# Mixer A: the delta rule's matrix reads the key gram from an SBUF copy instead of a second set of matmuls

## The chip, the cores and the metric

One core of one Trainium2 chip runs one inference step of a two-layer diffusion backbone. The metric is the device time of the core in microseconds. Shown are the median of three runs and one further execution that the hardware profiler recorded. Engines are named as in the profile: PE is TensorE's matmul stream, PEld its weight loads, DVE is VectorE, ACT is ScalarE, POOL is GpSimd, SP is SyncE, whose queue issues the DMAs here.

## The reference, cut to what matters

640 tokens (128 of context, 512 latent) go through an even and an odd layer. In the even layer `p = h @ w_in` feeds eight gated-DeltaNet heads (mixer A) beside eight attention heads (mixer B), and both results go through `w_out`. A DeltaNet head works in chunks of 64 tokens, in two directions:

```python
def l2norm(x): return x * rsqrt(sum(x * x, -1) + EPS)
q = l2norm(q) * DK_A ** -0.5 ; k = l2norm(k)
...
decay = exp(where(tri, gc[..., :, None] - gc[..., None, :], NEG))
kb = k * beta[..., None]
lmat = where(strict, einsum('bhncd,bhnsd->bhncs', kb, k) * decay, 0.0)
tmat = lmat + eye(CHUNK)
u = triangular_solve(tmat, v * beta) ; w = triangular_solve(tmat, kb * exp(gc))
attn = where(tri, einsum('bhncd,bhnsd->bhncs', q, k) * decay, 0.0)
```

Three 64x64 products of each chunk matter here: keys with keys (for `lmat`), keys with queries (for `attn`), and the diagonals of keys with keys and of queries with queries (for the two norms). Keys and queries enter all of them without their norms; those are multiplied in later, per token.

## The kernel before, in words

**The big matmuls.** The projection of the even layer is cut into 53 blocks of 128 output features. `Main` works them off: a block has four quarters, a quarter's weights come by a DMA on SP's queue (`w_st`), are split by ACT into a high part (`w_hi`, L1049) and by DVE into a low part (`w_lo`, L1051), and are multiplied three times with the activations (`acc<-hh,w_hi`, `acc<-hl,w_hi`, `acc<-hh,w_lo`), 320 tokens at a time.

**The order on PE.** `run` puts the instructions of PE in an order written down at build time. Every mixer is a generator. A `yield` of a number asks to be continued that much later, by a planner's clock `g.now`, in which a matmul counts a fixed price (`G.mm`; ten products of a gram count 0.53 us together). Whenever no generator is due, `Main.step` emits a few of the big matmuls. PE keeps exactly this order; the instructions of the other engines are ordered by the compiler's own scheduler, within their data dependencies, and may be moved ahead of others there. Each engine then works strictly in its order.

**A head of mixer A.** `prep` takes the blocks of keys and queries, runs the short convolution (`a_conv`) and then `a_prep`, which the change touches. `a_prep` first asks for the gram of keys with keys and that of queries with queries: ten 64x64 products each, written by PE to a PSUM tile `a_gram`. DVE multiplies it with a unit matrix into half of the tile `a_M` or `a_at` (L268) and sums it (L269); that gives the norms. Norms, gates and decays then become small per-token factors on DVE, and the decay matrices `a_M` and `a_at`, made by DVE (L308, L309), ACT (L310, L311) and POOL (L300, L301, L314). After `yield LAT["gram"]` (9 us of planner time) PE computes keys with keys into a new `a_gram`, DVE multiplies it into `a_M` (L320), and `a_invert` sends `a_M` through DRAM to POOL (SP's queue, L481 and L484), which inverts triangles of 32x32 in 30 dependent pairs of steps. Then PE computes keys with queries, and DVE multiplies that into `a_at` (L320 again). About 50 us later the inverse is loaded (`a_inverted`), put together (`a_join`, tile `i_vps`), and `a_scan` walks the ten chunk steps of the head (tiles `a_st`, `a_vns`, `a_vno`, `a_s`). The scan of one head and the preparation of the next overlap, and both overlap the attention heads of mixer B (tiles `at_s`, `at_pt`, `at_o`).

**PSUM.** In this stage the eight banks are: three for `acc`, three for the scan, and two that everything else shares in turn (tag `"gen"`): `a_gram`, `at_s`, `at_pt`, `at_o`, `i_vps`, the transposes, and `ada_ps` of a side stream (`g.aside`) that computes modulations inside the scan. A new user of that pair waits until the last but one has been read.

Of the kernel before, what the change touches and what calls it, by code (L numbers as in the profile page):

```python
# [8 lines left out]
F32 = mybir.dt.float32  # L9
# [80 lines left out]
def rsqrt(g, pool, x, n, tag, bufs=1):  # L90

    nc = g.nc
    y = pool.tile([128, n], F32, name=f"{tag}_y", tag=f"{tag}_y", bufs=bufs)[0:x.shape[0]]
    t = pool.tile([128, n], F32, name=f"{tag}_t", tag=f"{tag}_t")[0:x.shape[0]]
    yi = y.bitcast(I32)
    nc.vector.tensor_scalar(out=yi, in0=x.bitcast(I32), scalar1=1, scalar2=None, op0=ALU.logical_shift_right)
    nc.vector.tensor_scalar(out=yi, in0=yi, scalar1=-1.0, scalar2=float(0x5F3759DF), op0=ALU.mult, op1=ALU.add)
    for _ in range(3):
        nc.vector.tensor_mul(t, y, y)
        nc.vector.scalar_tensor_tensor(out=t, in0=t, scalar=-0.5, in1=x, op0=ALU.mult, op1=ALU.mult)  # L100
        nc.vector.scalar_tensor_tensor(out=y, in0=t, scalar=1.5, in1=y, op0=ALU.add, op1=ALU.mult)
    return y
# [137 lines left out]
def a_prep(g, h, qT, kT):  # L240

    nc, c, A = g.nc, g.c, g.A
    W, P1 = g.paw, g.pa1
    U = [128, 2, 5]
    hs = lambda t: t[:, :, :, h]
    bc = lambda t, n: t.unsqueeze(3).to_broadcast([128, 2, 5, n])


    df = W.tile([128, 10, 64], F32, name="a_df", bufs=1)
    for lo, hi in HALVES:  # L250
        nc.sync.dma_start(df[lo:hi], g.gcd[:, :, h, lo:hi].rearrange("o b s -> (o b) s").unsqueeze(0).to_broadcast([64, 10, 64]))
    b10 = lambda t: t.unsqueeze(2).to_broadcast([128, 10, 64])
    at = g.pe.tile([128, 2, 5, 64], F32, name="a_at", tag="a_at", bufs=2)
    M = P1.tile([128, 2, 5, 64], F32, name="a_M")
    def gram(x):

        ps = g.psg.tile([128, 5, 64], F32, name="a_gram", tag="gen")
        for b in range(5):
            for hf in range(2):
                cc = b * 128 + hf * 64  # L260
                g.mm(ps[hf * 64:hf * 64 + 64, b], lhsT=x[0][:, cc:cc + 64], rhs=x[1][:, cc:cc + 64], start=True, stop=True,
                     tile_position=(0, hf * 64))
        return ps

    ss = W.tile([128, 2, 5], F32, name="a_ss")
    for i, (x, sq) in enumerate(((kT, M), (qT, at))):
        ps = gram((x, x))
        nc.vector.tensor_tensor(out=sq[:, 0], in0=ps, in1=c["i64"].unsqueeze(1).to_broadcast([128, 5, 64]), op=ALU.mult)  # L268
        nc.vector.tensor_reduce(out=ss[:, i], in_=sq[:, 0], op=ALU.add, axis=mybir.AxisListType.X)  # L269
        yield  # L270
    sse = W.tile([128, 2, 5], F32, name="a_sse")
    nc.vector.tensor_scalar_add(sse, ss, 4 * EPS)
    rr = rsqrt(g, W, sse.rearrange("p a b -> p (a b)"), 10, "a_rr", bufs=2)
    rk, rq = rr[:, 0:5], rr[:, 5:10]
    rkb = rk.unsqueeze(1).to_broadcast(U)

    sm = lambda n: W.tile(U, F32, name=n, bufs=2)
    fm = c["fm"].rearrange("p (o b) -> p o b", o=2)
    bm = c["bm"].rearrange("p (o b) -> p o b", o=2)
    a = W.tile(U, F32, name="a_a")  # L280
    rk2 = W.tile([128, 5], F32, name="a_rk2")
    nc.vector.tensor_mul(rk2, rk, rk)
    nc.vector.tensor_mul(a, hs(A["beta"]), rk2.unsqueeze(1).to_broadcast(U))
    p2 = sm("a_p2")
    nc.vector.tensor_mul(p2, bm, sse[:, 0].unsqueeze(1).to_broadcast(U))
    nc.vector.tensor_add(p2, p2, hs(A["bfm"]))
    nc.vector.scalar_tensor_tensor(out=p2, in0=p2, scalar=0.5, in1=rkb, op0=ALU.mult, op1=ALU.mult)
    p1 = sm("a_p1")
    nc.vector.tensor_mul(p1, a, fm)
    nc.vector.tensor_add(p1, p1, bm)  # L290
    nc.vector.scalar_tensor_tensor(out=p1, in0=p1, scalar=-1.0, in1=hs(A["egc"]), op0=ALU.mult, op1=ALU.mult)
    c1 = sm("a_c1")
    nc.vector.tensor_mul(c1, a, bm)
    nc.vector.tensor_add(c1, c1, fm)
    c2 = sm("a_c2")
    nc.vector.tensor_mul(c2, c1, hs(A["dl"]))


    d4 = df.rearrange("p (o b) s -> p o b s", o=2)
    nc.gpsimd.tensor_tensor(out=d4, in0=d4, in1=bc(hs(A["gc"]), 64), op=ALU.subtract)  # L300
    nc.gpsimd.tensor_tensor(out=at, in0=df.rearrange("p (o b) s -> p o b s", o=2),  # L301
                            in1=c["maskA"].rearrange("p (o s) -> p o s", o=2).unsqueeze(2).to_broadcast([128, 2, 5, 64]),
                            op=ALU.add)
    Mu = M.rearrange("p o b s -> p (o b) s")
    for o, (lo, hi) in enumerate(HALVES):
        f, b = slice(o * 5, o * 5 + 5), slice(5 - o * 5, 10 - o * 5)
        ms = c["maskS"][lo:hi].unsqueeze(1).to_broadcast([64, 5, 64])
        nc.vector.scalar_tensor_tensor(out=Mu[lo:hi, f], in0=df[lo:hi, f], scalar=-1.0, in1=ms, op0=ALU.mult, op1=ALU.add)  # L308
        nc.vector.tensor_tensor(out=Mu[lo:hi, b], in0=df[lo:hi, b], in1=ms, op=ALU.add)  # L309
    nc.scalar.activation(M, M, AF.Exp)  # L310
    nc.scalar.activation(at, at, AF.Exp)  # L311
    an = W.tile([128, 10], F32, name="a_an")
    nc.vector.tensor_scalar_mul(an, a.rearrange("p o b -> p (o b)"), -1.0)
    nc.gpsimd.tensor_tensor(out=Mu, in0=Mu, in1=b10(an), op=ALU.mult)  # L314


    yield LAT["gram"]
    for dst, x in ((M, kT), (at, qT)):
        ps = gram((kT, x))
        nc.vector.tensor_tensor(out=dst, in0=ps.unsqueeze(1).to_broadcast([128, 2, 5, 64]),  # L320
                                in1=dst, op=ALU.mult)
        if dst is M:
            inv = a_invert(g, M)
        yield
    return dict(h=h, qT=qT, kT=kT, inv=inv, at=at, p1=p1, p2=p2, c1=c1, c2=c2, rq=rq)
# [149 lines left out]
def a_invert(g, M):  # L475

    nc, W, P1 = g.nc, g.paw, g.pa1
    d1 = g.pd.tile([6, 10, 32, 32], F32, name="inv_in", tag="inv_in")
    for q in range(4):
        sub = q % 2  # L480
        nc.sync.dma_start(d1[q].rearrange("u i j -> i u j"),  # L481
                          M[q * 32:q * 32 + 32].rearrange("p o b s -> p (o b) s")[:, :, sub * 32:sub * 32 + 32])
        if sub == 1:
            nc.sync.dma_start(d1[4 + q // 2].rearrange("u i j -> i u j"),  # L484
                              M[q * 32:q * 32 + 32].rearrange("p o b s -> p (o b) s")[:, :, 0:32])
    SY = P1.tile([128, 1024], F32, name="i_S").rearrange("p (i j) -> p i j", i=32)
    S, Yt = SY[0:40], SY[64:104]
    nc.sync.dma_start(S, d1[0:4].rearrange("q u i j -> (q u) i j"))
    E = nc.gpsimd
    E.memset(S.rearrange("p i j -> p (i j)")[:, 0:1024:33], 1.0)  # L490
    for j in range(1, 31):
        n = 31 - j
        t = P1.tile([40, 240], F32, name="i_tmp", bufs=2)[:, 0:n * j].rearrange("p (a b) -> p a b", a=n)
        E.tensor_tensor(out=t, in0=S[:, j + 1:, j].unsqueeze(2).to_broadcast([40, n, j]),  # L494
                        in1=S[:, j, 0:j].unsqueeze(1).to_broadcast([40, n, j]), op=ALU.mult)
        E.tensor_tensor(out=S[:, j + 1:, 0:j], in0=S[:, j + 1:, 0:j], in1=t, op=ALU.add)  # L496
    Y = S
    E.tensor_tensor(out=Yt, in0=Y.rearrange("p i j -> p j i"), in1=g.c["ones"][0:40, 0:32].unsqueeze(1).to_broadcast([40, 32, 32]),
                    op=ALU.mult)
    d2 = g.pd.tile([2, 4, 10, 32, 32], F32, name="inv_out", tag="inv_out")  # L500
    nc.sync.dma_start(d2[0].rearrange("q u i j -> (q u) i j"), Y)
    nc.sync.dma_start(d2[1].rearrange("q u i j -> (q u) i j"), Yt)
    return d1, d2
# [1044 lines left out]
def body(nc, tc, I, O):  # L1548
    off = [(k, v.shape[1]) for k, v in const_table().items()]
    with ExitStack() as es:  # L1550
# [100 lines left out]
        with ExitStack() as e1:  # L1651
# [25 lines left out]
            def prep():  # L1677
                for h in range(8):
                    yield lambda: st["joined"] >= h - 2
                    k = a_conv(g, h, 1, (yield from get(8 + h, 0.5)))  # L1680
                    yield lambda: st["scanned"] >= h - 2
                    q = a_conv(g, h, 0, (yield from get(h, 0.5)))
                    yield LAT["conv"]
                    yield lambda: st["gates"]
                    prepped[h] = yield from a_prep(g, h, q, k)
                    st["ready"][h] = g.now
# [299 lines left out]
```

## Time and profile before

| | before |
|---|---|
| median of three runs | 2717.81 us (2716.46 to 2723.16) |
| the profiled execution | 2723.34 us, span 2721.5 us |
| mean granted PE clock | 0.983 |
| busy: PE, PEld | 2601.2 us (96%), 2435.2 us (89%) |
| busy: DVE, ACT, POOL | 1536.9 us (56%), 954.0 us (35%), 704.9 us (26%) |
| matmuls of `a_gram` | 640 of 21303, between 189.3 and 974 us |
| mixers A and B | from about 180 to 1240 us |

A busy share is an average over the whole span. PE's matmuls overlap one another, so the time that a group costs is read from the distance of the starts, not from the sum of the durations. A row of the timeline gives start, duration, engine, line, instruction, `out<-in`, shape and count; the brackets at its end say how long the engine had been idle before it and who ended the wait. In the trace one of the kernel's fp32 products shows as two matmul records, so a gram of ten products shows as 20.

### The profile page before, as it was taken

How to read it: one execution, taken by the hardware profiler on the slowest of the kernel's cores; microseconds unless marked ns; L12 is line 12 of the kernel's file. 1: busy time of each engine (PE TensorE's matmuls, PEld its weight loads, DVE VectorE, ACT ScalarE, POOL GpSimd, SP SyncE). 2: the span in 40 equal slices, each digit the busy share in tenths (PEclk: the TensorE clock that was granted, in tenths of full speed). 3: DMA queues.
4: the chain of work that ended last, by engine and by line, in shares of the span. 5: the costliest groups of instructions: out<-in, count | busy, mean ns of one | idle time of the engine just before them, and what ended most of it. 6: DMA issues, size and time to landing. Idle time of an engine off the chain costs nothing.

```text
span 2721.5 us, 54637 instructions
## 1 busy us (share of the span) xinstructions
PE 2601.2 (96%) x21303; PEld 2435.2 (89%) x21303; DVE 1536.9 (56%) x3598; ACT 954.0 (35%) x2150; POOL 704.9 (26%) x894
## 2 busy tenths in 40 slices
PE   6989999999999999999999899999999999999996
PEld 4779788988978997799998899999999999998996
DVE  5766546656556565357876755546453644545225
ACT  3232343433433343442224443343333434233222
POOL 2326514253251550001223330012001301221113
PEclk9989999999999999999999999999999999999998
DMA  9932434243243424246653413323232222325324
GB/s 334 309 97 71 116 95 122 81 133 116 85 126 111 123 60 136 72 143 200 214 186 115 127 64 105 106 76 97 81 108 90 87 93 87 98 69 183 99 97 136
DMA packets 264706, 329.85 MB, mean 121 GB/s; under 512 B 76013, under 2 KB 148925, under 8 KB 264447
## 3 DMA queue, kind: packets, MB, share of 16 engines
q1 hardware_dynamic: 264447, 326.35, 38.2%
q8 instruction: 168, 2.75, 0.4%
q14 instruction: 91, 0.75, 0.1%
HBM read 294.95 MB, written 28.68 MB: 119 GB/s over the span
## 4 chain that ended last, share of the span: by engine, by line
PE 44%; DVE 3%; DMA 2%; issue 1%; ACT 0%; DVEq 0%; SPq 0%; ACTq 0%
PE acc L77 38%; PE at_s L77 1%; PE at_o L77 1%; DMA vec<-w_ada 1%; PE c_lv L77 1%; DVE hl L1774 1%; DVE vec L1320 1%; PE c_ops L77 1%; PE tm_ps L84 1%; PE c_U L77 0%; DVE x L1427 0%; PE at_pt L84 0%; DVE w_lo L1051 0%; PE c_bp L77 0%; DMA hl<-o_d 0%
## 5 line engine op out<-in xcount | busy, mean ns | idle before, releaser
L77 PE MATMUL acc<-hh,w_hi 128*128 128x320 f32 (+1 forms) x4544 | 1446.7, 319 | 18.7 <-ACT w_hi L1049 5.7
L77 PE MATMUL acc<-hl,w_hi 128*128 128x320 f32 (+1 forms) x4544 | 1415.6, 312 | 7.7 <-DVE hl L1229 7.7
L77 PE MATMUL acc<-hh,w_lo 128*128 128x320 f32 x4480 | 1394.4, 311 | 4.8 <-DVE w_lo L1051 4.8
L77 PEld LDWEIGHTS acc<-hh,w_hi 128*128 128x128 f32 (+1 forms) x4544 | 856.5, 189 | 59.8 <-issue 32.8
L77 PEld LDWEIGHTS acc<-hl,w_hi 128*128 128x128 f32 (+1 forms) x4544 | 857.5, 189 | 12.9 <-DVE hl L1229 11.0
L77 PEld LDWEIGHTS acc<-hh,w_lo 128*128 128x128 f32 x4480 | 847.3, 189 | 7.4 <-DVE w_lo L1051 6.7
L1051 DVE TENSOR_TENSOR w_lo<-w_st,w_hi 128x512 fp32r<-128x512 f32 x561 | 439.1, 784 | 588.1 <-ACT w_hi L1049 578.5
L1049 ACT CAST w_hi<-w_st 128x512 fp32r<-128x512 f32 (+1 forms) x604 | 365.2, 605 | 925.1 <-PE acc L77 783.9
L1320 DVE SCALAR_TENSOR_TENSOR vec<-vec,cond 128x256 f32<-128x256 f32 (+1 forms) x360 | 212.3, 634 | 23.3 <-DMA vec<-w_ada 21.5
L496 POOL TENSOR_TENSOR i_S<-i_S,i_tmp 40x30 f32<-40x30 f32 (+14 forms) x240 | 141.1, 588 | 18.7
L494 POOL TENSOR_TENSOR i_tmp<-i_S 40x30 f32<-40x30 f32 (+14 forms) x240 | 134.2, 559 | 18.0
L1463 POOL TENSOR_TENSOR n_acc<-n_acc,n_sq 128x640 f32<-128x640 f32 (+1 forms) x30 | 45.9, 1530 | 298.2 <-ACT n_sq L1462 298.2
L77 PE MATMUL ada_ps<-adv,cond 128*32 128x128 f32 x2048 | 94.7, 293 | 25.4 <-DMA adv<-w_ada 24.9
L929 POOL TENSOR_TENSOR c_X<-c_b 128x320 f32<-128x320 f32 x56 | 46.1, 822 | 221.9 <-PE c_lv L77 195.0
L77 PEld LDWEIGHTS ada_ps<-adv,cond 128*32 128x32 f32 x2048 | 48.7, 113 | 53.5 <-DVE n_acc L1463 19.4
L215 DVE SCALAR_TENSOR_TENSOR a_y<-a_pad,consts,a_y 128x644 f32<-128x644 f32 x96 | 89.7, 934 | 2.2
L790 POOL TENSOR_TENSOR d_bias<-d_braw,d_mask 128x256 f32<-128x256 f32 x32 | 27.9, 905 | 231.8 <-PE tm_ps L84 90.7
L1287 DVE TENSOR_TENSOR adv<-adv,ada_ps 128x128 f32<-128x128 f32 x144 | 40.5, 281 | 73.3 <-PE ada_ps L77 72.4
L301 POOL TENSOR_TENSOR a_at<-a_df,consts 128x640 f32<-128x640 f32 x8 | 13.7, 1712 | 253.9 <-DVE a_ss L269 222.0
L665 POOL TENSOR_TENSOR b_sw<-b_sw,b_tab 128x512 f32<-128x512 f32 x10 | 14.9, 1491 | 234.8 <-DMA b_sw<-b_q 199.7
L404 ACT ACTIVATE a_ot<-a_st,g_egc 128x128 f32<-128x128 f32 x72 | 26.4, 367 | 107.2 <-PE a_st L77 105.7
L1051 POOL TENSOR_TENSOR w_lo<-w_st,w_hi 128x256 fp32r<-128x256 f32 (+1 forms) x43 | 36.3, 851 | 106.6 <-ACT w_hi L1049 89.0
(310 smaller groups left out, 2760.6 us busy)
## 6 DMA issues: line engine op xcount, KB each, us to landing
adv<-w_ada SPq DMA_DIRECT2D x256, 256.0 KB
w_st<-w_in_odd SPq DMA_DIRECT2D x232, 256.0 KB
w_st<-w_in_even SPq DMA_DIRECT2D x188, 256.0 KB
w_st<-w_out_even SPq DMA_DIRECT2D x72, 256.0 KB
w_st<-w_out_odd SPq DMA_DIRECT2D x72, 256.0 KB
vec<-w_ada SPq DMA_DIRECT2D x64, 256.0 KB
vec<-w_ada SPq DMA_DIRECT2D x128, 128.0 KB
hl<-o_d SPq DMA_DIRECT2D x31, 320.0 KB
```

Of the source, the lines that this page charges most:

```text
L77: i = self.nc.tensor.matmul(out, lhsT=lhsT, rhs=rhs, **kw)
L84: i = self.nc.tensor.transpose(out, x, ident)
L215: nc.vector.scalar_tensor_tensor(out=y, in0=pad[:, j:j + CL], scalar=w[:, j:j + 1], in1=y, op0=ALU.mult, op1=ALU.add)
L494: E.tensor_tensor(out=t, in0=S[:, j + 1:, j].unsqueeze(2).to_broadcast([40, n, j]), in1=S[:, j, 0:j].unsqueeze(1).to_broadcast([40, n, j]) ...
L496: E.tensor_tensor(out=S[:, j + 1:, 0:j], in0=S[:, j + 1:, 0:j], in1=t, op=ALU.add)
L790: nc.gpsimd.tensor_tensor(out=bias[:, j], in0=braw[:, :, x0:x0 + 32], in1=g.dmask[:, j * 32:j * 32 + 32].unsqueeze(1).to_broadcast([128, 8 ...
L929: nc.gpsimd.tensor_tensor(out=pv(X[0])[:, :, 1 - d], in0=bv[:, :, 1 - d], in1=bm, op=ALU.subtract)
L1049: nc.scalar.copy(hi, st)
L1051: (nc.gpsimd if g.spare >= 0 else nc.vector).tensor_tensor(out=lo, in0=st, in1=hi, op=ALU.subtract)
L1287: nc.vector.tensor_add(acc, acc, ps)
L1320: nc.vector.scalar_tensor_tensor(out=acc[:, c], in0=st, scalar=sc, in1=acc[:, c], op0=ALU.mult, op1=ALU.add)
L1463: eng.tensor_add(accs[0][:, cs], accs[0][:, cs], t[:, cs])
```

## The change

The gram of keys with keys that `a_prep` computes for the norms is copied by ACT from PSUM to a new SBUF tile `a_kk` (five blocks of 64 columns on 128 partitions, fp32). After `yield LAT["gram"]` the multiplication into `a_M` takes this tile; the second gram of keys with keys is gone. The gram of keys with queries stays. Both multiplications of L320 keep their place in the program, and `a_invert` follows the first as before.

```diff
     ss = W.tile([128, 2, 5], F32, name="a_ss")
+    kk = W.tile([128, 5, 64], F32, name="a_kk")
     for i, (x, sq) in enumerate(((kT, M), (qT, at))):
         ps = gram((x, x))
+        if x is kT:
+            nc.scalar.copy(kk, ps)
         nc.vector.tensor_tensor(out=sq[:, 0], in0=ps, in1=c["i64"].unsqueeze(1).to_broadcast([128, 5, 64]), op=ALU.mult)
         nc.vector.tensor_reduce(out=ss[:, i], in_=sq[:, 0], op=ALU.add, axis=mybir.AxisListType.X)
         yield
...
     yield LAT["gram"]
-    for dst, x in ((M, kT), (at, qT)):
-        ps = gram((kT, x))
+    for dst in (M, at):
+        ps = kk if dst is M else gram((kT, qT))
         nc.vector.tensor_tensor(out=dst, in0=ps.unsqueeze(1).to_broadcast([128, 2, 5, 64]),
                                 in1=dst, op=ALU.mult)
         if dst is M:
```

## The prediction

> **What bounds the kernel now.** I read the engines' busy time, then the stretch of mixers A and B by windows, then the grams' weight loads head by head in the timeline.
>
> ```profile
> PE 2601.2 (96%) x21303; PEld 2435.2 (89%) x21303; DVE 1536.9 (56%) x3598; ACT 954.0 (35%) x2150; POOL 704.9 (26%) x894
> ...
> 180.00:980.00 800.00, 770.50 (x7103) 683.76 (x7103) 478.29 (x1251) 288.85 (x738) 306.38 (x465) 0.98 0.36 104
> 300.00:420.00 120.00, 117.03 (x1089) 99.11 (x1087) 62.57 (x176) 47.06 (x129) 39.16 (x64) 1.00 0.38 114
> 540.00:660.00 120.00, 117.59 (x1163) 101.03 (x1161) 74.69 (x186) 41.95 (x107) 44.75 (x68) 1.00 0.43 123
> ```
>
> In a window row the second number is its length, the third PE's busy time. PE is busy for 770.5 of the 800 us in which all grams lie, DVE for 478, ACT for 289. The big matmuls fill every gap, so a microsecond off PE's order is one off the time, unless the next thing in that order isn't ready.
>
> **The PE work removed.** 160 of 640 gram matmuls go, with their weight loads. Matmuls overlap, so a gram is priced by the distance from its first weight load to that of the next gram:
>
> ```profile
> 208.62 1.15 PEld L77 LDWEIGHTS a_gram<-a_o 128*64 128x64 f32 x20 [0.33 <-issue]
> 209.64 1.19 PEld L77 LDWEIGHTS a_gram<-a_o,a_o 128*64 128x64 f32 x20
> ...
> 437.23 0.66 PEld L77 LDWEIGHTS a_gram<-a_o 128*64 128x64 f32 x20 [0.20 <-PE a_st L77]
> 438.11 0.66 PEld L77 LDWEIGHTS a_gram<-a_o,a_o 128*64 128x64 f32 x20 [0.22 <-DVE adv L1287]
> ...
> 874.29 0.66 PEld L77 LDWEIGHTS a_gram<-a_o 128*64 128x64 f32 x20 [0.20 <-issue]
> 874.87 0.67 PEld L77 LDWEIGHTS a_gram<-a_o,a_o 128*64 128x64 f32 x20
> ...
> 972.84 0.66 PEld L77 LDWEIGHTS a_gram<-a_o 128*64 128x64 f32 x20 [0.19 <-issue]
> 973.42 0.67 PEld L77 LDWEIGHTS a_gram<-a_o,a_o 128*64 128x64 f32 x20
> ```
>
> That is 1.02 us in head 0, 0.88 in head 2 (with a wait for a PSUM buffer) and 0.58 in heads 6 and 7; heads 1, 3, 4 and 5 have 0.58 too. 1.02 + 0.88 + 6 x 0.58 = 5.38 us.
>
> **Head 0 keeps less of it.** PE later stands still for this head's inverse:
>
> ```profile
> 207.55 1.34 POOL L314 TENSOR_TENSOR a_M<-a_M,a_an 128x640 f32<-128x640 f32 x1 [4.24 <-DVE a_p L290]
> ...
> 208.85 0.47 DVE L603 TENSOR_SCALAR at_S<-at_S,at_den 128x512 f32<-128x512 f32 x1
> 210.07 0.82 DVE L320 TENSOR_TENSOR a_M<-a_gram,a_M 128x640 f32<-128x640 f32 x1 [0.75 <-PE a_gram L77]
> ...
> 273.63 0.31 PE L77 MATMUL i_vps<-i_X,i_M 32*32 32x32 f32 x2 [4.27 <-DMA i_X<-inv_out]
> ```
>
> What PE saves at 209 only lengthens the 4.27 us stall at 273, except as far as the inverse comes earlier. It does: the multiplication into `a_M` no longer waits for a gram. POOL's factor is done at 208.89, DVE is free at 209.32, so it starts 0.75 us earlier, and the way through SP's queue and POOL moves along. I take 0.7; the ends are 0 and 1.02.
>
> **A stall in head 7 goes.** The removed gram also held one of the two shared PSUM buffers:
>
> ```profile
> 975.02 0.82 DVE L320 TENSOR_TENSOR a_M<-a_gram,a_M 128x640 f32<-128x640 f32 x1
> ...
> 975.89 0.14 PEld L84 LDWEIGHTS at_pt<-consts,at_S 128*128 128x128 f32 x1 [1.29 <-DVE a_M L320]
> ```
>
> The transposes `at_pt` want the buffer of keys-with-keys, which is free only when DVE has multiplied it. Afterwards they take the other one, which was free when keys-with-queries began in it at 973.42. Late next could be `at_o`, which then needs the buffer of keys-with-queries; one multiplication of DVE, not two, stands before its release, so I expect it in time. A new group costs about 0.19 us anyway (0.19 and 0.20 "issue" above), so 1.1 us goes; ends 0 and 1.29.
>
> **The copy added: eight on ACT, 128x320, PSUM to SBUF.** ACT has room at this place, but see who reads PSUM together:
>
> ```profile
> 967.16 0.42 ACT L640 COPY b_vT<-acc 128x320 f32<-128x320 f32 x1
> ...
> 751.86 0.49 DVE L268 TENSOR_TENSOR a_M<-a_gram,consts 128x320 f32<-128x320 f32 x1 [1.23 <-PE a_gram L77]
> ...
> 754.99 0.34 DVE L409 TENSOR_SCALAR a_vns<-a_st,a_c 128x128 f32<-128x128 f32 x1
> ...
> 752.88 0.37 ACT L404 ACTIVATE a_ot<-a_st,g_egc 128x128 f32<-128x128 f32 x1 [3.34 <-PE a_st L77]
> ...
> 755.37 0.37 ACT L411 ACTIVATE a_vno<-a_st,a_c 128x128 f32<-128x128 f32 x1 [0.37 <-DVE a_vns L409]
> ...
> 534.55 0.20 PEld L77 LDWEIGHTS a_st<-a_vno,a_at 64*64 64x64 f32 x4 [0.53 <-ACT a_vno L411]
> ...
> 755.79 0.20 PEld L77 LDWEIGHTS a_st<-a_vno,a_at 64*64 64x64 f32 x4 [0.53 <-ACT a_vno L411]
> ...
> 864.04 0.19 PEld L77 LDWEIGHTS a_st<-a_vno,a_at 64*64 64x64 f32 x4 [0.53 <-ACT a_vno L411]
> ...
> ACT a_vno L411 <- DVE a_vns L409: 51.6, 55, 2.9
> ```
>
> ACT had been idle for 3.34 us before 752.88, so a copy from 751.86 costs ACT nothing. But L409 and L411 only read the same PSUM tile, neither uses the other's result, and still ACT waits for DVE, 55 times: two engines' readings of one PSUM tile are put one after the other, in program order. The copy stands first in the program, so DVE's L268 waits for it: 0.42 us and a hop of 0.04 (755.33 to 755.37), 0.46 us.
>
> DVE works nine instructions without a gap from L268 through L409, so `a_vns`, then ACT's `a_vno`, then PE's `a_st` come 0.46 us later, where PE waits 0.53 already. Heads 3 to 6 look alike here (first, third and last shown): 4 x 0.46 = 1.84 us lost. In the other heads I count nothing. The ends are 0 and 8 x 0.46 = 3.68.
>
> [...]
>
> **The multiplication into `a_M`** now has both operands in SBUF. The nearest row:
>
> ```profile
> L1229 DVE TENSOR_TENSOR hl<-hl,hh 128x640 fp32r<-128x640 f32 x31 | 25.1, 821 | 10.3 <-ACT hh L1228 10.1
> ...
> 763.11 0.59 DVE L426 SCALAR_TENSOR_TENSOR a_s<-a_s,g_egl,a_st 128x128 f32<-128x128 f32 x2
> ...
> 765.10 0.20 PEld L77 LDWEIGHTS a_st<-a_s,a_wT 128*64 128x64 f32 x4 [0.19 <-DVE zs_a L236]
> ```
>
> 0.82 us, as with one operand in PSUM: no term of its own. The scheduler may put it right behind L314, some 4 us earlier; then it stands ahead of the scan's `a_s`, done at 763.70 and wanted at 765.10: 1.4 us of cover for 0.82. If that cover were gone, up to 0.82 us a head would show. SP's DMAs of `a_invert` go out as many as before and move along; the weight loads they would pass are issued quarters ahead of need.
>
> **Sum.** 0.7 + 0.58 + 0.88 + 4 x 0.58 + 0.58 + 1.1 - 1.84 = 4.3 us gained. Against the profiled execution (2723.34 us: the span of 2721.5 and 1.8 around it) that makes 2719.0. This execution lies 5.5 us above the median; 2717.81 - 4.3 = **2713.5 us**, 0.16% less.
>
> **The order is laid anew.** The planner counts 0.53 us less a head, so the streams meet the big matmuls at other places. The two stretches of 120 us quoted first have different meetings and idle for 2.97 and 2.41 us, 0.56 apart. Over the 1060 us of both mixers (180 to 1240), if it went one way throughout, 5 us in either direction, an estimate. It is larger than any term above.
>
> **Rivals.**
>
> *More than the sum, 2712 to 2707.* The copy delays nothing on PE's path (6.2 us) and the new order meets fewer stalls (up to 5): 6 to 11 us gained. For it: the waits at 273 and for `a_vno` leave that much to win. Against: nothing directs the order that way.
>
> *No gain, about 2718.* The saving is lost where the mixers end, since the last head of B and the reloading of the heads' outputs set that time, not PE:
>
> ```profile
> 1210.00:1220.00 10.00, 9.59 (x71) 9.08 (x69) 7.21 (x12) 6.74 (x16) 0.00 (x0) 1.00 1.00 354
> 1220.00:1230.00 10.00, 7.69 (x48) 7.72 (x49) 8.53 (x20) 7.22 (x15) 0.00 (x0) 0.83 0.51 171
> 1230.00:1240.00 10.00, 7.79 (x45) 7.34 (x45) 5.92 (x10) 5.19 (x13) 0.00 (x0) 0.83 0.48 149
> ```
>
> For it: PE idles for 4.9 of these 30 us. Against: the last head's query block comes out of the same queue of big matmuls, which ends earlier.
>
> *Slower, 2725 to 2728.* DVE is held up by POOL:
>
> ```profile
> 754.85 1.64 POOL L301 TENSOR_TENSOR a_at<-a_df,consts 128x640 f32<-128x640 f32 x1 [53.73 <-DVE a_ss L269]
> 761.27 1.28 POOL L314 TENSOR_TENSOR a_M<-a_M,a_an 128x640 f32<-128x640 f32 x1 [4.79 <-DVE a_p L290]
> 767.94 1.28 POOL L300 TENSOR_TENSOR a_df<-a_df,g_gc 128x640 f32<-128x640 f32 x1 [5.39 <-DMA a_df<-gc_d]
> ...
> 755.25 1.78 DVE L1051 TENSOR_TENSOR w_lo<-w_st,w_hi 128x512 fp32r<-128x512 f32 x1
> ...
> 291.15 0.69 DVE L1051 TENSOR_TENSOR w_lo<-w_st,w_hi 128x512 fp32r<-128x512 f32 x1
> ```
>
> A subtraction with two SBUF operands takes 0.69 us, but 1.78 when it starts under POOL's L301: it ends after POOL does. The new multiplication is of that kind. Held for 1.28 to 1.64 us in each head, with PE waiting for the scan operand behind it, and with the copy's 0.46, it costs 13.9 to 16.8 against 6.2: 2725.5 to 2728.4. From 6.2 / 8 = 0.77 us a head on PE's path it decides the sign. Against: POOL is idle for the 5.39 us between L314 and L300, where it would run.
>
> [...]
>
> **Chances.** Two runs of this kernel tell about 0.3%, 8 us, from no change. The sum as worked out, 0.45: within. More than the sum, 0.30: 0.23 of it where the order gives over 2 us (past 8 in all), 0.07 within. No gain, 0.14: within. Slower, 0.11. That the change removes nothing is excluded by the diff. Faster by over 0.3%: 0.23; within: 0.66; slower: 0.11. The range goes from the largest gain, 2717.8 - 11.2 less 1.4 for the runs' own spread downwards, 2705, to 2723, where all eight copies are on the path (-2.5), the order costs 5 and the runs' spread adds some; the slower rival is left out.
>
> **What the profile afterwards would show.** `a_gram`: 480 matmuls. In heads 1 and 3 to 6 one gram of 0.58 us behind `yield`. L268 of `a_M` starting 0.46 us later after its gram, released by ACT's copy, and PE's wait for `a_vno` there near 1 us. No wait of 1.29 us at `at_pt`. L320 of `a_M` 0.82 us, 3 to 4 us ahead of the other. `i_vps` waiting no longer than 4.6 us in head 0. PE's idle time in 180 to 980 at 29.5 us, give or take 5. The prediction is wrong if L320 of `a_M` is stretched by POOL, if copies come late in ACT's order, or if the mixers' end doesn't move.

## The result, and the profile after

| | before | after |
|---|---|---|
| median of four runs each, same chip | 2718.12 us (2716.46 to 2723.16) | 2749.98 us (2748.95 to 2754.24) |
| the profiled execution | 2723.34 us, span 2721.5 | 2748.95 us, span 2747.2 |

The ratio is 1.0117, 95% interval 1.010 to 1.0135: 32 us slower, where 4 us less was forecast. The lines of the changed kernel are numbered three higher from the first gram on: L268 became L271, L300 L303, L308 and L309 L311 and L312, L314 L317, L320 L323, L409 L412, L411 L414, L426 L429. The copy is L270. Pins and edits in the experiments shift the numbers by a few more.

Read first the same windows as before (length, then PE, PEld, DVE, ACT and POOL busy, then the granted PE clock):

```profile
180.00:980.00 800.00, 751.50 (x6725) 663.57 (x6724) 453.97 (x1194) 282.64 (x723) 298.77 (x462) 0.96 0.35 102
300.00:420.00 120.00, 118.13 (x1110) 99.65 (x1107) 63.20 (x176) 48.26 (x131) 38.48 (x64) 1.00 0.37 112
540.00:660.00 120.00, 111.82 (x1018) 96.55 (x1019) 67.90 (x185) 40.38 (x102) 41.58 (x66) 0.94 0.36 106
```

PE idles for 48.5 of the 800 us, not 29.5, and 540 to 660 has a clock of 0.94. Where no head is prepared (300 to 420) nothing is lost. The loss sits where heads are prepared beside a scan. Next, the waits of the changed kernel from 180 to 1260 (us in total, times, longest):

```profile
DVE a_M L323 <- POOL a_M L317: 39.6, 6, 7.4
PE a_st L77 <- ACT a_vno L414: 27.0, 11, 5.7
```

and the one of the kernel before that answers to the second:

```profile
PE a_st L77 <- ACT a_vno L411: 5.0, 10, 1.1
```

The first has no counterpart before: DVE's multiplication into `a_M` then waited only for PE's gram (2.1 us in all). One such place, in the preparation of head 3, in the timeline of the changed kernel:

```profile
534.61 1.67 POOL L304 TENSOR_TENSOR a_at<-a_df,consts 128x640 f32<-128x640 f32 x1 [44.08 <-DVE a_ss L272]
549.78 1.27 POOL L303 TENSOR_TENSOR a_df<-a_df,g_gc 128x640 f32<-128x640 f32 x1 [13.49 <-DMA a_s<-state_delta]
551.01 1.26 POOL L317 TENSOR_TENSOR a_M<-a_M,a_an 128x640 f32<-128x640 f32 x1
...
537.21 0.59 SPq L251 DMA_DIRECT2D a_df<-gc_d  x1
540.29 1.40 SPq L251 DMA_DIRECT2D a_df<-gc_d  x1
...
542.33 0.17 DVE L316 TENSOR_SCALAR a_an<-a_a 128x10 f32<-128x10 f32 x1
552.30 0.83 DVE L323 TENSOR_TENSOR a_M<-a_kk,a_M 128x640 f32<-128x640 f32 x1 [7.40 <-POOL a_M L317]
553.24 0.35 DVE L412 TENSOR_SCALAR a_vns<-a_st,a_c 128x128 f32<-128x128 f32 x1
...
553.62 0.37 ACT L414 ACTIVATE a_vno<-a_st,a_c 128x128 f32<-128x128 f32 x1 [7.33 <-DVE a_vns L412]
554.04 0.69 PE L77 MATMUL a_st<-a_vno,a_at 64*64 64x128 f32 x4 [5.70 <-ACT a_vno L414]
```

and the same place of POOL before:

```profile
533.61 1.64 POOL L301 TENSOR_TENSOR a_at<-a_df,consts 128x640 f32<-128x640 f32 x1 [44.82 <-DVE a_ss L269]
540.04 1.29 POOL L314 TENSOR_TENSOR a_M<-a_M,a_an 128x640 f32<-128x640 f32 x1 [4.79 <-DVE a_p L290]
546.80 1.28 POOL L300 TENSOR_TENSOR a_df<-a_df,g_gc 128x640 f32<-128x640 f32 x1 [5.47 <-DMA a_df<-gc_d]
```

POOL's order is another. Before, the scaling of this head's `a_M` (L314) comes first and the subtraction for the *next* head (L300, which needs that head's `a_df` from DRAM) second. After the change the subtraction (L303) stands first. Its two loads were issued at 537.21 and 540.29, and POOL sits idle until 549.78. (The row puts the end of that wait down to a load of `a_s`, issued behind them; the subtraction doesn't read `a_s`, so when `a_df` itself landed isn't seen in this head. In the swaps of heads 1 and 2 the row names `a_df`.) The scaling, whose factor `a_an` was there from 542.5 on, ends at 552.27. DVE stands at its multiplication into `a_M` for 7.40 us, and behind it in DVE's order is `a_vns` of the running scan; ACT's `a_vno` waits for that, and PE for `a_vno`. The swap is there in heads 1 to 6 of eight (counted from 0).

PE paid twice for this stall. Windows of 10 us of the changed kernel (length, PE busy, clock), and weight loads from its timeline:

```profile
540.00:550.00 10.00, 8.35 (x90) 1.00 0.57 177
550.00:560.00 10.00, 5.96 (x45) 0.66 0.41 89
560.00:570.00 10.00, 10.00 (x96) 1.00 0.53 155
...
556.14 0.33 PEld L77 LDWEIGHTS acc<-hl,w_hi 128*128 128x128 f32 x1
557.74 0.33 PEld L77 LDWEIGHTS acc<-hl,w_hi 128*128 128x128 f32 x1
558.39 0.19 PEld L77 LDWEIGHTS acc<-hl,w_hi 128*128 128x128 f32 x1
```

After the stall weight loads take 0.33 us instead of 0.19 until about 558.2, four microseconds after PE went on. In windows of 1 us the granted clock is 1.00 from 548 to 551 us, 0.68 from 551 to 552 (PE idle since 548.34), 0.50 from 552 to 558, 0.90 from 558 to 559 and then 1.00.

From 180 us to the wait for `at_S` in which the mixers end (before, then after):

```profile
180.00:1222.31 1042.31, 1002.71 (x9151) 0.99 0.35 105
...
180.00:1251.55 1071.55, 1008.80 (x8979) 0.97 0.34 102
```

The stretch is 29.2 us longer: 23.1 us more idle time, 22.0 of which are the waits for `a_vno`, and 6.1 more busy time, with 172 matmul records fewer (160 of them the 80 products of the removed grams) but a clock of 0.97 instead of 0.99.

### The profile page after: what moved, and what is told of

Its sections match the earlier page's. It is cut to its first block, busy times and chain, and to the rows that moved or that the text cites. A ratio compares the mean times of both kernels' runs of the same rounds, so it can differ in the third digit from the quotient of the medians.

```text
span 2747.2 us, 54331 instructions
## 1 busy us (share of the span) xinstructions
PE 2606.9 (95%) x21143; PEld 2439.6 (89%) x21143; DVE 1536.3 (56%) x3598; ACT 957.5 (35%) x2158; POOL 696.0 (25%) x894
## 5 line engine op out<-in xcount | busy, mean ns | idle before, releaser
L1054 DVE TENSOR_TENSOR w_lo<-w_st,w_hi 128x512 fp32r<-128x512 f32 x561 | 427.4, 763 | 573.4 <-ACT w_hi L1052 569.5
L77 PEld LDWEIGHTS ada_ps<-adv,cond 128*32 128x32 f32 x2048 | 48.5, 113 | 56.1 <-DVE n_acc L1466 20.0
L304 POOL TENSOR_TENSOR a_at<-a_df,consts 128x640 f32<-128x640 f32 x8 | 13.6, 1697 | 252.1 <-DVE a_ss L272 252.1
```

The source lines that it names most:

```text
L77: i = self.nc.tensor.matmul(out, lhsT=lhsT, rhs=rhs, **kw)
L1054: (nc.gpsimd if g.spare >= 0 else nc.vector).tensor_tensor(out=lo, in0=st, in1=hi, op=ALU.subtract)
```

## The experiments

Theory 1: the loss is POOL's order, with the late load in front of the scaling and DVE's strict order behind it. Theory 2: the copy holds up DVE. Theory 3: the planner, which counts 0.53 us less a head, lays PE's order anew for the worse. `issue_after` in the diffs keeps an instruction behind a named one on its engine and adds no wait. The experiments were timed beside the kernel before in three series, and their us are compared with the median before of the same series: 2715.90 for e1 to e4, 2718.82 for e8, e9, e15 and e17, 2719.29 for e13, e16, e18 and e21.

| kernel | POOL's scaling | DVE: `a_M`, `a_vns` | median us | ratio (95%) |
|---|---|---|---|---|
| changed | late, 6 heads | `a_M` first | 2749.98 | 1.0117 (1.010 to 1.0135) |
| e1 POOL pinned | in time | `a_M` first | 2720.74 | 1.0019 (1.0007 to 1.0032) |
| e2 unused copy | late, 6 heads | `a_vns` first | 2743.53 | 1.0111 (1.0095 to 1.0127) |
| e3 one gram, no copy | in time | `a_vns` first | 2712.68 | 0.9991 (0.9982 to 1.0000) |
| e4 copy late | in time | `a_M` first | 2731.42 | 1.0059 (1.0046 to 1.0072) |
| e17 `a_vns` first, copy late | in time | `a_vns` first | 2718.43 | 0.9998 (0.9988 to 1.0009) |
| e8 POOL pinned, copy late, planner | in time | `a_M` first | 2721.20 | 1.0015 (1.0006 to 1.0025) |
| e15 `a_vns` first | late, 6 heads | `a_vns` first | 2743.78 | 1.0090 (1.0075 to 1.0105) |
| e9 before, swapped | late, 6 heads | `a_vns` first | 2738.64 | 1.0080 (1.0067 to 1.0092) |
| e21 `a_df` by POOL's queue | late, 7 heads | `a_M` first | 2757.00 | 1.0135 (1.0106 to 1.0164) |
| e13 two `a_df` | late, 5 heads | `a_M` first | 2742.55 | 1.0074 (1.0053 to 1.0095) |
| e16 `a_vns` first, POOL pinned | in time | `a_vns` first | 2718.67 | 1.0000 (0.9986 to 1.0015) |
| e18 `a_vns` first, copy late, two `a_df` | in time | `a_vns` first | 2719.34 | 0.9995 (0.9982 to 1.0008) |

"Late" counts heads in which DVE's multiplication into `a_M` waits 0.8 us or more for POOL. The orders in the third column are those of most heads.

**e1: POOL's order put back, and nothing else.**

```diff
-    nc.gpsimd.tensor_tensor(out=d4, ..., op=ALU.subtract)
+    with (g.tc.issue_after(g.scaled) if h else ExitStack()):
+        nc.gpsimd.tensor_tensor(out=d4, ..., op=ALU.subtract)
...
-    nc.gpsimd.tensor_tensor(out=Mu, in0=Mu, in1=b10(an), op=ALU.mult)
+    g.scaled = nc.gpsimd.tensor_tensor(out=Mu, in0=Mu, in1=b10(an), op=ALU.mult).ins
```

> The changed kernel, with one thing pinned: on POOL a head's subtraction (a_df) may not be issued ahead of the head before's scaling of a_M. The copy, the one gram, and VectorE's order (multiplication into a_M ahead of a_vns in six heads) stay as in the changed kernel. Theory 1 (the loss is the swap on POOL: the scaling stands behind a subtraction that waits for a DMA, VectorE's in-order queue waits for the scaling with a_vns behind it, PE waits for a_vno): time falls from 2750 to 2712-2722 us, VectorE's 7 us waits for POOL before the a_M multiplication are gone, PE's waits for a_vno fall from about 56 us to 13 or less. Theory 2 (the copy on ScalarE holds up VectorE, 1.7 us in each of 8 heads): stays at 2740-2752. Theory 3 (0.53 us less TensorE time per head in the mixers' planner lays their work anew): stays at 2740-2752.

Measured 1.0019: of the 1.17% only 0.19% is left, 5 us. DVE's waits for POOL are gone, and POOL's order is that of before again. Head 3 in the timeline, then two of the waits of this kernel:

```profile
535.01 1.27 POOL L318 TENSOR_TENSOR a_M<-a_M,a_an 128x640 f32<-128x640 f32 x1 [6.33 <-DVE a_p L293]
541.92 1.27 POOL L304 TENSOR_TENSOR a_df<-a_df,g_gc 128x640 f32<-128x640 f32 x1 [5.64 <-DMA a_s<-state_delta]
...
PE a_st L77 <- ACT a_vno L415: 7.8, 10, 1.2
DVE a_M L271 <- ACT a_kk L270: 13.2, 8, 2.2
```

The waits for the copy are all still there. Theories 2 and 3 are out as the cause of the large loss: the copy and the planner's new price are in this kernel too.

**e2: the copy alone, in the kernel before.**

```diff
         ps = gram((x, x))
+        if x is kT:
+            nc.scalar.copy(kk, ps)
```

> The kernel before, with the copy of the first gram added on ScalarE and not used: the second gram of the keys is still computed and still multiplied into a_M from PSUM. By the instruction order, POOL is swapped as in the changed kernel, but VectorE has a_vns ahead of the a_M multiplication as before. Theory 1 (both are needed: the late scaling, and a_vns behind the instruction that waits for it): the scaling is 7-11 us late in six heads but a_vns is not held; 2718-2735 us, taken 2724, PE's waits for a_vno near the 13 us of before. Theory 2 (the copy's hold on VectorE): 2740-2760. Theory 3 (planner): 2715-2721, as the planner is told the same TensorE work as before.

Measured 1.0111, 2743.53 us: a miss for theory 1 as I had stated it, and inside the range that theory 2 gave for this kernel. What excludes theory 2 is e1, which has the same waits for the copy and is 23 us faster. POOL was swapped as expected, so the copy alone brings the swap about, used or not. But `a_vns` ahead of the multiplication saved next to nothing. The waits and the timeline of this kernel:

```profile
DVE a_M L323 <- POOL a_M L317: 25.0, 6, 5.6
PE ada_ps L77 <- DVE a_M L323: 15.3, 5, 4.1
...
553.36 0.83 DVE L323 TENSOR_TENSOR a_M<-a_gram,a_M 128x640 f32<-128x640 f32 x1 [5.58 <-POOL a_M L317]
554.25 0.59 PE L77 MATMUL ada_ps<-adv,cond 128*32 128x128 f32 x8 [4.11 <-DVE a_M L323]
```

The gram sits in one of the two shared PSUM buffers until the late multiplication has read it, and PE's `ada_ps`, next for that buffer, stands for 4 us. So a late scaling costs by whatever is next: here a buffer, in the changed kernel `a_vns`. (The granted clock in 550 to 560 is 0.83 here.)

**e3: one gram, no copy.** `a_M` is multiplied with the gram of keys and queries; the second gram of keys with keys is left out, so the kernel doesn't compute the layer and serves for the price alone.

```diff
-    for dst, x in ((M, kT), (at, qT)):
-        ps = gram((kT, x))
+    for dst in (M, at):
+        ps = gram((kT, qT)) if dst is M else ps
```

> The kernel before without the second gram of the keys and without a copy: both multiplications (into a_M and a_at) read the one gram of keys with queries from PSUM, so a_M is multiplied with the wrong gram; all else is as before. It prices TensorE's work alone. By the instruction order POOL and VectorE stand as before. Theory 1: 2711-2716 us (5.4 us less, the gram's 80 matmuls). Theory 2: the same. Theory 3 (the planner's clock, 0.53 us less per head, re-lays the mixers for the worse): 2735-2752.

Measured 0.9991: 2.4 us less by the ratio, between 0 and 4.9. Theory 3 is out for good, since the planner counts the same 0.53 us less here. The gain is smaller than the 5.4 us worked out, which lie just above the interval.

**e4: the copy behind DVE's reads of the gram.**

```diff
-        if x is kT:
-            nc.scalar.copy(kk, ps)
         nc.vector.tensor_tensor(out=sq[:, 0], in0=ps, ...)
         nc.vector.tensor_reduce(out=ss[:, i], in_=sq[:, 0], ...)
+        if x is kT:
+            nc.scalar.copy(kk, ps)
```

> The changed kernel with the copy placed behind VectorE's multiplication and sum of the first gram (it reads PSUM after them instead of before). By the instruction order POOL is then as in the kernel before (scaling ahead of the next head's subtraction), VectorE has the a_M multiplication ahead of a_vns. Theory 1: 2710-2720 us, some 0-5 below the kernel with only POOL pinned (the VectorE's wait of 1.7 us a head for the copy is gone). Theory 2 (copy's hold on VectorE): 2708-2716, and then the kernel with only POOL pinned stays near 2745. Theory 3: stays at 2740-2752.

Measured 1.0059: POOL in time, as the order said, but 11 us above theory 1's range. The trace shows a second place of the same kind:

```profile
538.53 1.28 POOL L303 TENSOR_TENSOR a_df<-a_df,g_gc 128x640 f32<-128x640 f32 x1 [4.85 <-DMA adv<-w_ada]
...
544.46 0.48 DVE L312 TENSOR_TENSOR a_M<-a_df,consts 64x320 f32<-64x320 f32 x1 [3.71 <-DMA i_M<-inv_in]
544.96 0.49 DVE L311 SCALAR_TENSOR_TENSOR a_M<-a_df,consts 64x320 f32<-64x320 f32 x1
545.48 0.61 DVE L429 SCALAR_TENSOR_TENSOR a_s<-a_s,g_egl,a_st 128x128 f32<-128x128 f32 x2
...
545.88 0.73 PE L77 MATMUL a_st<-a_s,a_wT 128*64 128x128 f32 x3 [3.54 <-DVE a_s L429]
...
PE a_st L77 <- DVE a_s L429: 11.9, 4, 4.5
```

DVE's two mask instructions of the next head (L312, L311) stand ahead of `a_s` in four heads; L312 waits 3.71 us for a DMA of the inverse (presumably until `a_M` has been sent out by `a_invert`; the subtraction was done at 539.81), and PE waits for `a_s`. In the kernel before, and in e1, they stand behind `a_s`.

**e17: both orders of DVE put back, copy late.** The multiplication into `a_M` is emitted one step later, beside that into `a_at`, and pinned behind the last `a_vns`:

```diff
+        if dst is M:
+            yield
+            continue
+        for dst, ps in ((M, kk), (at, gram((kT, qT)))):
+            with (g.tc.issue_after(g.vns) if dst is M and h else ExitStack()):
+                nc.vector.tensor_tensor(out=dst, in0=..., in1=dst, op=ALU.mult)
```

> The changed kernel with the copy behind VectorE's reads of the first gram, and the multiplication into a_M pinned on VectorE behind the a_vns emitted before it (and emitted one step later, beside that into a_at). By the instruction order POOL is as before the change, and VectorE's order of a_vns, a_s, a_M, a_at and the next head's a_M mask is that of before, head by head. If orders alone were the loss (theory 1, widened: every instruction on VectorE that hangs on a DMA or on POOL and is set ahead of a_vns or a_s costs PE its wait), what is left is the gram's gain: 2709-2715 us, ratio 0.997-1.000, as the kernel with one gram and no copy (2712.7). Rival (the copy itself, 0.43 us of ScalarE and SBUF in place of PSUM as operand, costs): 2720-2731, as with the late copy alone.

Measured 0.9998: the whole loss is gone, and it is level with the kernel before. It ends inside the expected ratio, 3 us above the expected time (the kernel before measured 2.9 us more in this series than in the first). The rival's 2720 to 2731 would be 1.0015 to 1.0056 beside the 2715.90 of the first series, above the interval.

**e8: POOL pinned, copy late, and the planner charged for the removed gram** (`g.now += 10 * 64 * 4 / 4800` in its place, with the pins of e1 and the copy of e4):

> The changed kernel with three things: POOL's scaling pinned ahead of the next head's subtraction, the copy behind VectorE's reads, and the mixers' planner still charged 0.53 us for the gram that is gone. By the instruction order VectorE has a_M ahead of a_vns, as with the late copy alone, but the next head's two mask instructions on a_M stand behind a_s again (with the late copy alone they stood ahead of a_s in heads 3 to 6, and PE waited there 3.5, 2.3, 4.5 and 1.6 us for a_s). If that place is what the late copy alone lost against the one-gram kernel (2731.4 against 2712.7): 2711-2718. Rival (a_M ahead of a_vns is itself the loss, 0.8 us of VectorE in front of the a_vns): 2722-2731.

Measured 1.0015, 2721.20 us: between the two expected ranges and in neither. The masks stand behind `a_s` again, PE's waits for `a_s` fall from 11.9 to 3.9 us, and 12 us of e4's 16 are gone (1.0059 to 1.0015). So that place was most of e4's loss; the pin and the planner's charge that e8 adds aren't told apart from it. But it stays above e17: with `a_M` ahead of `a_vns` 0.15 to 0.19% is lost (e8 1.0015, e1 1.0019), with `a_vns` first nothing (e17 0.9998, e16 1.0000). The pairs differ by 0.0017, give or take 0.0014, and by 0.0019, give or take 0.0019, so this loss is only just told from none. (e8 and e17 differ by the pin and the charge too, e16 and e1 by the place of the multiplication, and of `a_invert` behind it, alone.)

**e15: `a_vns` first, POOL still swapped** (the edit of e17 without the late copy):

> The changed kernel with only the multiplication into a_M put behind a_vns on VectorE (emitted one step later and pinned). POOL stays swapped, the copy stays ahead. Theory 1 as first stated (the late scaling costs only through a_vns standing behind the waiting multiplication): 2712-2722. Theory 1 widened (the scaling is 7 us late and VectorE's queue waits for it wherever the multiplication stands: a_at's multiplication with the PSUM slot of its gram and a_s are behind it now): 2735-2748, as the kernel with the unused copy (2743.5), and PE's waits move from a_vno to a_s or to the PSUM slot.

Measured 1.0090, as theory 1 widened has it. DVE still stands for 28.2 us at the multiplication; PE's waits for `a_vno` fall to 11.0 us and those for `a_s` rise to 8.7 (before: 5.0 and 3.9), 10.8 us more than before; where the rest of the 25 us lies wasn't worked out:

```profile
DVE a_M L327 <- POOL a_M L317: 28.2, 6, 6.2
PE a_st L77 <- ACT a_vno L418: 11.0, 9, 3.3
PE a_st L77 <- DVE a_s L433: 8.7, 6, 2.4
```

**e9: the swap without the change.** The kernel before, with the next head's load and subtraction emitted ahead of this head's scaling, which is pinned behind them:

```diff
+    if h < 7:
+        g.df[h + 1] = a_front(g, h + 1)      # load of a_df, subtraction
...
-    nc.gpsimd.tensor_tensor(out=Mu, in0=Mu, in1=b10(an), op=ALU.mult)
+    g.tc.keep_in_program_order(nc.gpsimd.tensor_tensor(out=Mu, in0=Mu, in1=b10(an), op=ALU.mult))
```

> The kernel before, without any of the change (two grams, no copy), but with the next head's load and subtraction of a_df emitted before this head's scaling of a_M, which is pinned behind it on POOL: POOL's order is that of the changed kernel in heads 1 to 6 (and in head 0 as well). If the swap alone is enough: 2733-2748, VectorE waiting some 5-8 us for POOL at the a_M multiplication in each such head. If it needs the change's other parts: 2715-2722.

Measured 1.0080: slower by 20 us (22 by the ratio) with none of the change in it. The place is only partly the expected one: DVE's waits for POOL add up to 13.7 us, and are at most 1.1 us in heads 3 to 6. The rest lies elsewhere: the first head already ends 5.3 us later, and PE's waits for the DMA of `adv` are 10.9 us instead of 2.7.

```profile
DVE a_M L331 <- POOL a_M L325: 13.7, 6, 4.2
PE ada_ps L77 <- DMA adv<-w_ada: 10.9, 7, 2.7
```

The edit moves the `a_df` loads too, so e9 shows that an early subtraction is dear and not by itself that the waiting scaling is why.

**e21: `a_df` loaded from POOL's queue** (`nc.gpsimd.dma_start` for `nc.sync.dma_start`):

> The changed kernel with one edit: a_df is loaded by DMAs that POOL issues, not SP, whose queue has adv, w_st and new_state_delta transfers ahead of it (in the changed kernel the two halves of head 4's a_df are issued by SP at 537.2 and 540.3 and POOL starts on them at 549.8). By the instruction order POOL still has the next head's subtraction ahead of the scaling in heads 3 to 6 (no longer in 1 and 2), and VectorE's order is that of the changed kernel. If the landing of a_df is what makes the swap dear: VectorE's wait for the scaling falls from 7 us to 0-4 us in heads 3 to 6 and the time to 2716-2730. Rival (the swap itself, 1.3 us of subtraction ahead of the scaling and the order around it): waits stay at 6-8 us, 2738-2750.

Measured 1.0135, slower than the change itself. The load came later, not sooner:

```profile
542.16 1.66 POOL L304 TENSOR_TENSOR a_at<-a_df,consts 128x640 f32<-128x640 f32 x1 [44.09 <-DVE a_ss L272]
545.30 0.75 POOL L251 DMA_DIRECT2D a_df<-gc_d  x1 [1.49 <-DVE a_sse L275]
552.21 0.72 POOL L251 DMA_DIRECT2D a_df<-gc_d  x1 [6.15 <-issue]
558.79 1.28 POOL L303 TENSOR_TENSOR a_df<-a_df,g_gc 128x640 f32<-128x640 f32 x1 [5.86 <-DMA a_df<-gc_d]
560.03 1.26 POOL L317 TENSOR_TENSOR a_M<-a_M,a_an 128x640 f32<-128x640 f32 x1
```

POOL issued the second half 6.9 us after the first, for no reason that the profile shows. The scaling then ran 17.9 us after the mask addition began (changed kernel: 16.4), DVE waited 47.6 us in all instead of 39.6, and the time rose. In heads 0 to 2 the subtraction isn't ahead here, and the scaling is late all the same (DVE waits 6.35, 3.73 and 2.85 us): POOL's own second DMA issue stands in front of it. So an earlier load wasn't had, but the dependence shows from the other side: a later scaling, whatever makes it late, and a larger loss.

**e13: two buffers for `a_df`** (`bufs=2`):

> The changed kernel with two buffers for a_df in place of one. By the instruction order this doesn't bring the scaling forward: POOL then has the subtraction of the head after next ahead of this head's scaling, and that load waits for VectorE's last read of the buffer, two heads earlier in its turn, as late as before. If the order and the late load are the cause: 2738-2752, VectorE's waits for POOL at a_M still 5-8 us in six heads. Rival (one buffer too few is the cause): 2712-2722.

Measured 1.0074, 2742.55 us, in the range. POOL's subtraction now runs a further head ahead and still stands before the scaling, released as late as before (549.91 in the place of 549.78); DVE waits 32.6 us in five heads.

**e16: `a_vns` first and POOL pinned, copy ahead**, to price the wait for the copy:

> The changed kernel with both orders pinned (POOL's scaling ahead of the next head's subtraction; the multiplication into a_M behind a_vns) and the copy left ahead of VectorE's first read, which waits 1.7 us a head for it. Beside the kernel with a_vns first and a late copy (ratio 0.9998) it prices that wait: if VectorE has room for it, ratio 0.998-1.001; if it is on the path in most heads, some 13 us in all, ratio 1.003-1.005.

Measured 1.0000 against 0.9998 with the copy late: a difference of 0.0002, give or take 0.0018 from the two intervals. DVE's wait for the copy has room, as far as 5 us can be seen.

**e18: e17 with two `a_df`.**

> The kernel with a_vns first and the late copy, with two a_df buffers. By the instruction order POOL has each subtraction a head earlier, ahead of the mask addition of the head before, so that POOL never stands at a late load with a scaling behind it. If the load's lateness still costs something in the orders of before (POOL idle for a_df there 42 us, VectorE's mask behind it): 2710-2716, ratio 0.997-0.999. If the subtraction has room: ratio 0.999-1.001.

Measured 0.9995 (0.9982 to 1.0008): no gain beside e17. Beside e3, which leaves a gram out, no kernel here beats the kernel before.

**What adds up.** By the ratios: one gram less -0.09% (e3); the copy and the rest that separates e3 from e16 +0.09%, not told from zero; `a_M` ahead of `a_vns` +0.19% (e16 to e1); POOL's swap +0.98% (e1 to the changed kernel), 27 us. With the scaling late the five kernels that carry a copy lose 0.7 to 1.35%, wherever DVE's multiplication stands. With it in time and the masks behind `a_s`, none loses over 0.2% by its median ratio (e1's interval reaches 0.32%). That is shown. What the compiler's scheduler counted when it swapped POOL's order isn't; the runs say only that the copy ahead of DVE's reads brings the swap about, and the copy behind them doesn't.

## Why the prediction was wrong

The step that failed stands in the part on the multiplication into `a_M`: "The scheduler may put it right behind L314, some 4 us earlier; then it stands ahead of the scan's `a_s` ...: 1.4 us of cover for 0.82. If that cover were gone, up to 0.82 us a head would show." The place was right, in DVE's order it now stands ahead of the scan. The price took for granted that L314 stays where it was on POOL. I treated only PE's order as new and let the scheduler move DVE's instruction and nothing on POOL, although POOL's order is the scheduler's too. The row that held the price was on the page: L300 in the quoted rows had waited 5.39 us for its `a_df` after L314. Put L300 first, and that wait, the 1.28 us of the subtraction and the idle time until then all stand in front of the scaling. The runs showed that in place of the 0.82 us: DVE waited 5.6 to 7.4 us for POOL in each of six heads, 39.6 us in all, and putting L317 back in front of L303, nothing else, took 27 us off (e1). Where its operand was ready (e1, e8), the early multiplication did cost about 0.15 to 0.19%, 4 to 5 us and only just told from nothing, near the size given for the lost cover (0.82 us in six to eight heads).

Point by point:

- *The PE work removed*: 480 matmul records of `a_gram` are left, as said. Its 5.38 us were measured as 2.4 us in e3 (0 to 4.9). Where the rest is isn't settled; single executions differ by more.
- *Head 0*: the inverse comes earlier, far more than the 0.7 us: `i_vps` waits 0.43 us at 269.69 instead of 4.27 at 273.63. 1.65 us of the 3.9 were there ahead of the first gram (`gc_t` at 186.86 instead of 188.51), so that much isn't the change's. At the end of the head nothing is left of it (366.66 against 366.75 us, the first `zs_a`). In between lies the preparation of head 1, the first with the swap: DVE waits 5.65 us for POOL before 292.26, and PE 1.54 us for `a_vno` at 294.80. The rest of the 3.8 us lost there isn't laid out.
- *Head 7's stall*: gone; the `at_pt` behind that gram starts at 1000.69 without a wait.
- *The copy*: DVE's read waits for it in all eight heads (`DVE a_M L271 <- ACT a_kk L270`: 13.3 us in all, the wait for the gram included). L271 in head 5 waits 1.69 us where L268 had waited 1.23 in the quoted row: 0.46 us, the term to the hundredth. That this reaches PE (1.84 us) can't be seen (e16 beside e17). My later "1.7 us a head" for the same wait wrongly included the wait for the gram.
- *The multiplication itself*: 0.82 us expected, 0.811 to 0.826 measured.
- *The order laid anew by the planner*: 5 us either way had been allowed; e3, with the planner's new price, shows no loss. The new order that mattered was the scheduler's.
- *The rival "slower"*: right in sign and in its words "DVE is held up by POOL", wrong in mechanism and size. It was priced at 1.28 to 1.64 us a head, for a multiplication stretched as the `w_lo` subtraction beside POOL had been (1.78 us instead of 0.69); in the changed kernel L323 was never stretched (0.811 to 0.826 us), it waited up to 7.4 us for POOL's result.
- *The range*: it stopped at 2723 because no case moved an instruction on POOL.

The sign that I had named for "wrong", L320 of `a_M` stretched by POOL or a late copy, wouldn't have caught it; the wait in front of that instruction did.

## What to carry to other kernels

Where a compiler orders an engine's instructions, a small added instruction on one engine can change the order on another (here a copy of 0.43 us on ACT swapped POOL's order, e2); before pricing a move, ask for each in-order engine which instruction waiting for a DMA could come to stand in front of a short one that someone needs, and take the wait of that row as the price. After such a change, compare the order of every engine with the old one before anything else; a pin of one instruction took back 27 of the 32 us here. In this kernel 5.38 us of work off the busiest engine were worth 2.4 us (e3), while a single stall of 5.70 us cost PE its own length and then about 4 us at a clock of 0.50.

## What the runs showed of the hardware

- A PE stall of 5.70 us in the changed kernel was followed by about 4 us at a clock of 0.50 (0.66 in the 10 us around it).
- Two DMAs of 160 KB issued from POOL's queue one after the other: the second issue came 6.9 us after the first in e21, and such a wait (6.15 us in that row) stood there in all eight heads (48.7 us in total). The cause isn't known.
- The stretching of a DVE instruction beside POOL that the prediction's rival priced does appear, but in the changed kernel at another instruction: L311 takes 0.49 us (the median of 16), and 1.61 us where it starts under POOL's L304 (535.02 and 534.61). No run shows what stretches it.

```profile
535.02 1.61 DVE L311 SCALAR_TENSOR_TENSOR a_M<-a_df,consts 64x320 f32<-64x320 f32 x1
```

At the new multiplication it shows once in e16, in head 1: 1.62 us instead of 0.82 where it starts under POOL's subtraction (288.76 and 288.42). In the changed kernel the two didn't meet.

```profile
288.42 1.28 POOL L304 TENSOR_TENSOR a_df<-a_df,g_gc 128x640 f32<-128x640 f32 x1 [2.37 <-DMA a_df<-gc_d]
288.76 1.62 DVE L328 TENSOR_TENSOR a_M<-a_kk,a_M 128x640 f32<-128x640 f32 x1
```
